# A streaming layer step on one core: state update and difference of two maps at full width, memory products in one stretch

## The chip, the core and the metric

The kernel runs on one core of a Trainium2 chip. The core has a tensor engine (PE in the profile) that multiplies, three engines for elementwise work (VectorE, DVE; ScalarE, ACT; GpSimd, POOL), a sync engine (SP) that here only issues transfers, and 16 transfer engines (DMA). PE multiplies a stationary operand with a moving one: `mm(out, lhsT, rhs)` gives `lhsT`'s columns as the rows of `out`, in a bank of the accumulator memory (PSUM). A product is called full-width here where its result has 128 rows, and narrow where it has 64 or 32; in the profile that is `128*64` or `128*32` ahead of the moving shape. A float32 product is two passes of PE, and `x4` in a row of PE counts passes.

The metric is the device time of one execution in microseconds, the median of the runs.

## The reference

One step of a layer with three groups of heads for 1024 prompt tokens and for 8 batches of 16 decode tokens: differential attention (two softmax maps, the second subtracted with a factor lambda), a matrix memory with gates (mLSTM), and attention into 256 memory tokens. Cut to what the change touches:

```
# differential attention: 4 heads, two maps of 64, values of 128
p = softmax(s)                         # [b, h, map, q, k]
w = p[:, :, 0] - lam * p[:, :, 1]
o = einsum('bhqk,bkhd->bhqd', w, v)
# mLSTM state of a head: 64 x 64 matrix C, vector n; for each chunk
C = decay * C0 + einsum('s,sd,se->de', wS, k, v)
n = decay * n0 + einsum('s,sd->d', wS, k)
# memory attention: 4 heads of 64, 256 memory tokens
om = softmax(qm @ mem_k.T / 8) @ mem_v * silu(gm)
y = x + concat([oa, hb, om]) @ w_out
```

## The kernel before

Tokens lie in 9 tiles of 128: eight of the prompt and one that holds the 8 x 16 decode tokens (`DEC`). The projections run in phases: the four heads of the differential attention, the gates, the memory attention (M), the two head pairs of the mLSTM (B0, B1) and the output projection (O0, O1). A phase loads its weights in k-tiles, splits them in a high and a low part, and `feed` computes a token tile's projection (into banks named z or y) as 24 products of 128x512: `wh` with the high part of the inputs (`hth`), `wh` with their low part (`htl`), `wl` with `hth`. These are most of PE's instructions.

Behind each projection the later stages of the tiles before it are written. `mem_unit` (from L608) is the M stage: queries transposed, scores (`mpm`, L630 to L640), then the part that the change touches, L644 to L666: gates transposed, and for each of two head pairs four transposes of `mpm`, a copy of them to `mpt` by ScalarE (L656), and four products with the memory values `mv` of 64x128. `b_stages` (from L1085) is the mLSTM of a head pair: `mlstm_in`, `mlstm_scores`, the read-out, and the state update (L1105 to L1115): `kw` are the weighted keys of two heads, `vx` their values with a column of ones, `up` the sum that DVE adds to the decayed state `cs`.

The decode attention (`dec_attention`, from L814) runs beside B0 and B1, two steps for each of 8 batches. `scores` loads four key tiles `kc` (512 KB each) and multiplies them with the block-diagonal queries `qz`, 32 rows a head. `values` transposes the exponentials `se` to `ewt`, loads four value tiles `vc` and multiplies, 32 rows a head (head, map, query), copies the sum to `ems`, and a last product with the signed reciprocal sums `sr` subtracts the two maps: 64 rows of `oa` for one batch. `kc` and `vc` share a ring of seven buffers. `mem_decode` (from L912) does the decode tokens' attention into their memories in the phase O0, with key tiles `mkc`.

Nothing of the order is written by hand. Each engine executes its instructions in one order that a scheduler fixes when the program is built, from the code's order, from priorities (`ahead(n)`) and from its own estimates. SP issues transfers in that order, and a transfer that waits for its data holds those behind it. The transfers beside the change are: `mixd`, a tile's finished branch outputs, written to memory by the stages; `bgt`, the gates of a tile, read back; `mb`, a tile of mask rows; the stores of the decode state (`out_11`, `out_12`: L1078, L1079, the second one is the single column `n`) and of the prompt state (L1118, L1119, likewise); and `wraw`, weights as they come from memory.

Of the kernel before, what the change touches and what calls it, by code (L numbers as in the profile page):

```python
# [11 lines left out]
F32 = mybir.dt.float32  # L12
# [20 lines left out]
# columns of the relaid w_in: a head of A: q k v ga; ib fb gb; qm gm; a head pair of B: q k v ob  # L33
W_A, W_G, W_M, W_B = 0, 2048, 2312, 2824

# the phases of the projections: priority of the stages before a tile, of its weights and of its
# products; order of the passes for the first tile and the others; banks; engines of the weights' hi
# parts (even k, odd k); k whose lo part is made by Pool; engine that evacuates transposes
# [15 lines left out]
# steps of the decode attention after each tile of the head pairs of B  # L54
# [4 lines left out]
def hymba_step(ctx: ExitStack, tc: tile.TileContext, a: dict, o: dict):  # L59
# [47 lines left out]
    def bc(ap, n):  # L107
        """[p, ...] -> [p, ..., n], repeated along a new last axis"""
        return ap.unsqueeze(len(ap.shape)).broadcast_to(list(ap.shape) + [n])

    def rep(ap, n):
        """[p, ...] -> [p, n, ...], repeated along a new first free axis"""
        return ap.unsqueeze(1).broadcast_to([ap.shape[0], n] + list(ap.shape[1:]))
# [4 lines left out]
    def flat(ap):  # L118
        return ap.rearrange("p a b -> p (a b)")

    # ------------------------------------------------------------------ constants
# [13 lines left out]
    def rsqrt(dst, ss, n):  # L135
        """dst = (ss + n eps) ** -0.5, the reciprocal rms over sqrt(n); the gains carry sqrt(n)"""
        V.tensor_scalar(ss, ss, n * EPS, None, ALU.add)  # L137
        root(dst, ss)
# [15 lines left out]
    # mixed branch outputs and gates of a token tile, stabilisers, values of the new decode tokens  # L154
# [6 lines left out]
    def small_loads():  # L161
# [3 lines left out]
        # carried here: the roots of n, the halves of silu and sigmoid (written with tanh), and, in  # L165
        # the gain of q, 8 * 0.125 / slope of the next head
# [12 lines left out]
    def selectors():  # L179
        # e16[r, q] = (r % 16 == q); bm[r, b] = (r // 16 == b); par[r, i] = ((r // 16) % 2 == i)  # L180
        # h32[r, h] = (r // 32 == h); selc[r, (h, q)] = h32[r, h] * e16[r, q]
# [5 lines left out]
        # sgn[r] = 1 on the rows of map 0, -lam on those of map 1, rows (h, m, q)  # L187
# [6 lines left out]
    def split_T(src, hi, lo, n):  # L194
        """transpose n [128,128] column blocks of src, split into hi and lo [128, n, 128]"""
# [7 lines left out]
    # the tensor engine's clock rises while the first loads run  # L203
# [9 lines left out]
    def weights(w, c0, n, gain=None, spare=()):  # L213
        """columns c0 to c0 + n of a [1024, .] weight, as hi and lo k-tiles; gain scales its rows.
        spare: (pool, tag, bufs) for raw tiles, where there is room"""
# [67 lines left out]
    def norm_T(xt, xp, hi, lo, xT=None):  # L283
        """rms-normed rows (gain not yet applied), transposed and split"""
# [16 lines left out]
    # a token tile's projection is traced ahead of the later stages of the tiles before it  # L301
# [20 lines left out]
    # -------------------------------------------- memory keys and values  # L322
# [9 lines left out]
    # -------------------------------------------- differential attention, prompt  # L332
# [4 lines left out]
    def a_norm(z):  # L337
        """q and k of a head, both maps, over their rms (gains not yet applied)"""
# [16 lines left out]
    def a_post_dec(h, z):  # L355
        """decode tile: q into block-diagonal (m, d) x (b, m, q) stationaries, k transposed"""
# [22 lines left out]
    def a_post(h, t, z, grp):  # L379
        # dist is scaled by the slope, so the scores carry scale / slope  # L380
# [24 lines left out]
        # contraction over (hi, lo) of q in the first map, (lo, hi) in the second  # L405
# [11 lines left out]
    def a_unit(h, t, grp):  # L417
        """attention of one query tile, in two stages"""
# [29 lines left out]
        # the norm takes out the sum of the first map, but for its eps  # L448
# [23 lines left out]
    # -------------------------------------------- mLSTM gate rows: (tile, head) x token in tile  # L472
    R = 36

    def gate_rows():
        # in buffers of the next phase
# [16 lines left out]
        # decode rows restart at every batch  # L493
# [12 lines left out]
        # log_sigmoid(f) = min(f, 0) - log1p(exp(-|f|)), log1p(u) = 2 atanh(u / (2 + u))  # L506
# [27 lines left out]
        # running stabiliser over the prompt chunks, per head  # L534
# [48 lines left out]
    # -------------------------------------------- cross-attention into the memory  # L583
    def mem_q(z, gt):
        """reciprocal rms of the queries, gate"""
# [10 lines left out]
    def mem_dec_q(z):  # L596
        """decode tile: queries, transposed"""
# [10 lines left out]
    def mem_unit(t, z):  # L608
        # the scores are scaled by the reciprocal rms of q in the softmax; the keys carry q's gain
# [8 lines left out]
        # (hi, lo) of the even heads, (lo, hi) of the odd ones  # L618
# [24 lines left out]
        yield  # L643
        tg = bank("tp").rearrange("p (a k) -> p a k", a=4)  # L644
# [4 lines left out]
        av = bank("av")[:, 0:256].rearrange("p (c k) -> p c k", c=2)  # L649
        for pr in range(2):  # L650
            tp = bank("tp").rearrange("p (a k) -> p a k", a=4)
            for h2 in range(2):
                for kt in range(2):
                    PE.transpose(tp[:, h2 * 2 + kt], pm[:, 2 * pr + h2, kt * P:(kt + 1) * P], ident)
            pt = shp.tile([P, 4, P], F32, tag="wth", name="mpt", bufs=3)
            S.copy(pt, tp)  # L656
            for kt in range(2):
                for h2 in range(2):
                    mm(
                        av[h2 * 64:h2 * 64 + 64, pr], mv[:, kt, pr * 2 + h2], pt[:, h2 * 2 + kt],  # L660
                        kt == 0, kt == 1,
                    )
        # this part of the mixed tile stays transposed
# [43 lines left out]
    # memory keys and values, in buffers that the attention uses later  # L707
    def mem_stages(t):
        def run(z):
# [9 lines left out]
            # 8 of gqm for the 8 that the reciprocal rms of q lacks, times 0.125 of the softmax: none left  # L719
# [63 lines left out]
    # the input and forget gates and gb, behind the last head  # L783
# [27 lines left out]
    # -------------------------------------------- attention over the caches, decode  # L811
    NKD = 1040

    def dec_attention():  # L814
# [16 lines left out]
        oa = ep.tile([P, 4, P], F32, name="oa")  # L831

        def scores(b):
            """rows (h, m, q): exp of the scores over the 1040 keys, signed reciprocal sums"""
# [24 lines left out]
        def values(b, se, sm):  # L859
            sr = ep.tile([P, 64], F32, tag="sr", name="sr", bufs=4)  # L860
            V.tensor_scalar(sr, flat(selc), sm[:, 5:6], None, ALU.mult)
# [27 lines left out]
            # the two maps, weighted and subtracted: rows (h, q)  # L889
            rs = slice((b % 2) * 64, (b % 2) * 64 + 64)  # L890
            mm(avb[rs, P:2 * P], sr, ms)
            S.copy(oa[rs, b // 2, :], avb[rs, P:2 * P])  # L892
# [18 lines left out]
    # -------------------------------------------- attention over the memories, decode  # L911
    def mem_decode(md):  # L912
        """two batches at a time, rows (head, batch of the pair, query)"""
        # contraction over (batch of the pair, head dimension): block-diagonal stationaries
# [48 lines left out]
    # -------------------------------------------- mLSTM  # L963
    # masks over (s, t): prompt causal; decode causal within a batch
# [342 lines left out]
```

## Time and profile before

| | us |
|---|---|
| runs | 783.5, 783.51, 788.57 (median 783.51) |
| profiled execution, span | 774.3 |
| PE busy | 738.2 (95%) |
| DVE, ACT, POOL busy | 473.7, 333.4, 237.4 |
| bytes moved by transfers | 106.19 MB, mean 137 GB/s |

The span is what the profiler sees between the first and the last instruction. The run's time has 9.2 us more around it. A row of the timeline tells the start, the duration (that of a pipelined PE row reaches into the next), the engine, the line, the operation with its result and operands, and how many were joined in the row; in brackets stands the idle time before it and what ended it. For PE the distance from start to start is the better measure of what an instruction costs.

### The profile page before, as it was taken

Reading aid. Unit: us, or ns where it says so; the run is one execution under the profiler, and the core shown is the slowest. Engines: PE = TensorE matmul, PEld = TensorE weight load, DVE = VectorE, ACT = ScalarE, POOL = GpSimd, SP = SyncE. Lnnn points to the kernel's source line nnn. Section 1 sums busy time; section 2 is a strip of 40 time slices with the busy share of each in tenths; the row PEclk is TensorE's granted clock in tenths of the full one; section 3 lists DMA queues with packets and bytes.
Section 4 is the critical chain, followed back from the end, with each engine's and each line's share of the span. In section 5 each row is a group of like instructions: output and inputs, shape, how many; then the busy total and the mean of one; then the engine's idle time right before and its main releaser. Section 6 shows DMA issues by size and latency. Waiting matters only on the chain.

```text
span 774.3 us, 14523 instructions
## 1 busy us (share of the span) xinstructions
PE 738.2 (95%) x4976; PEld 599.9 (77%) x4976; DVE 473.7 (61%) x1466; ACT 333.4 (43%) x976; POOL 237.4 (31%) x332
## 2 busy tenths in 40 slices
PE   7998999999999999999999999899979997799998
PEld 6776788878888888998878776577747775578887
DVE  6788886677787778677575835347335347644111
ACT  6566634564664466555356532234223334200200
POOL 6653441323223223336313502111012036221500
PEclk9999999999999999999999999999989999999999
DMA  8733430151014112324002407979994728874422
GB/s 310 287 107 109 149 89 22 41 157 45 25 49 124 46 35 70 106 76 124 25 15 46 123 14 251 200 276 327 348 207 157 286 42 299 194 260 124 142 83 95
DMA packets 84387, 106.19 MB, mean 137 GB/s; under 512 B 16054, under 2 KB 52698, under 8 KB 84314
## 3 DMA queue, kind: packets, MB, share of 16 engines
q1 hardware_dynamic: 84314, 105.28, 44.2%
q8 instruction: 39, 0.64, 0.3%
q14 instruction: 34, 0.28, 0.1%
HBM read 86.01 MB, written 19.23 MB: 136 GB/s over the span
## 4 chain that ended last, share of the span: by engine, by line
PE 75%; DMA 9%; DVE 9%; issue 2%; ACT 2%; POOL 2%; SPq 0%; POOLq 0%; DVEq 0%; ACTq 0%
PE ps_z L95 39%; PE ps_y L95 15%; PE ps_s L95 9%; PE ps_av L95 5%; DMA kc<-in_kT_dram 4%; PE ps_tp L459 2%; DVE wl L238 2%; DMA mkc<-in_mkT_dram 1%; DMA wraw<-in_w_in_dram 1%; DMA bgt<-gated 1%; PE ps_tp L200 1%; PE ps_tp L867 1%; PE ps_tp L404 1%; DVE xT L294 1%; POOL asm L133 1%
## 5 line engine op out<-in xcount | busy, mean ns | idle before, releaser
L95 PE MATMUL ps_z<-wh,htl 128*128 128x512 f32 (+2 forms) x552 | 214.8, 391 | 0.1
L95 PE MATMUL ps_z<-wh,hth 128*128 128x512 f32 (+2 forms) x552 | 200.2, 394 | 4.4 <-ACT hth L280 2.1
L95 PE MATMUL ps_z<-wl,hth 128*128 128x512 f32 (+2 forms) x552 | 192.1, 387 | 0.0
L95 PEld LDWEIGHTS ps_z<-wh,hth 128*128 128x128 f32 x552 | 103.6, 190 | 25.5 <-ACT hth L280 2.4
L95 PEld LDWEIGHTS ps_z<-wh,htl 128*128 128x128 f32 x552 | 104.7, 190 | 18.9 <-DVE htl L281 0.8
L95 PEld LDWEIGHTS ps_z<-wl,hth 128*128 128x128 f32 x552 | 103.1, 189 | 18.6 <-issue 1.2
L95 PE MATMUL ps_y<-wh,htl 128*128 128x512 f32 (+2 forms) x176 | 65.6, 374 | 0.0
L95 PE MATMUL ps_y<-wh,hth 128*128 128x512 f32 (+2 forms) x176 | 62.9, 378 | 0.3 <-ACT oa L892 0.3
L133 POOL TENSOR_TENSOR asm<-asm,nhalf 128x4 f32<-128x4 f32 x36 | 39.6, 1100 | 74.4 <-DVE asm L137 58.8
L443 ACT ACTIVATE usx<-usx,usm 128x1024 f32<-128x1024 f32 (+7 forms) x64 | 49.7, 778 | 29.0 <-DVE usm L437 26.5
L95 PE MATMUL ps_y<-wl,hth 128*128 128x512 f32 (+2 forms) x176 | 61.3, 378 | 0.0
L238 DVE SCALAR_TENSOR_TENSOR wl<-wraw,gnm,wh 128x512 fp32r<-128x512 f32 (+1 forms) x62 | 47.0, 783 | 4.6 <-ACT wh L231 3.2
L231 ACT ACTIVATE wh<-wraw,gnm 128x512 fp32r<-128x512 f32 (+1 forms) x56 | 38.0, 706 | 18.2 <-DMA wraw<-in_w_in_dram 15.7
L95 PE MATMUL ps_s<-aqk 128*128 128x256 f32 (+1 forms) x160 | 42.0, 288 | 0.9 <-ACT aqk L412 0.9
L437 DVE CUSTOM_DVE_ANT_0 usx<-ps_s,tab 128x512 f32<-128x512 f32 (+3 forms) x64 | 37.0, 587 | 8.9 <-PE ps_s L95 7.5
L133 POOL TENSOR_TENSOR usm<-usm,nhalf 128x1 f32<-128x1 f32 x32 | 19.6, 612 | 72.3 <-DVE usm L467 67.9
L95 PE MATMUL ps_s<-akl,aqk 128*128 128x256 f32 (+1 forms) x160 | 41.0, 283 | 0.0
L95 PE MATMUL ps_av<-avg,wth 128*128 128x128 f32 x288 | 38.7, 276 | 0.2 <-DVE uot L469 0.2
L95 PEld LDWEIGHTS ps_av<-avg,wth 128*128 128x128 f32 x288 | 36.9, 191 | 2.5 <-ACT wth L460 0.6
L95 PEld LDWEIGHTS ps_y<-wh,hth 128*128 128x128 f32 x176 | 32.8, 188 | 5.8 <-ACT oa L892 0.6
L95 PEld LDWEIGHTS ps_y<-wl,hth 128*128 128x128 f32 x176 | 32.9, 188 | 5.5 <-DVE wl L238 0.3
L95 PEld LDWEIGHTS ps_y<-wh,htl 128*128 128x128 f32 x176 | 33.1, 188 | 5.0
(443 smaller groups left out, 1376.7 us busy)
## 6 DMA issues: line engine op xcount, KB each, us to landing
kc<-in_kT_dram SPq DMA_DIRECT2D x32, 512.0 KB, 8.9
vc<-in_cache_attn_v_dram SPq DMA_DIRECT2D x32, 512.0 KB, 6.8
wraw<-in_w_in_dram SPq DMA_DIRECT2D x56, 256.0 KB, 3.0
omx<-mixd SPq DMA_DIRECT2D x9, 512.0 KB, 4.1
out_dram<-oxt SPq DMA_DIRECT2D x17, 256.0 KB, 4.3
xt<-in_x_prompt_dram SPq DMA_DIRECT2D x8, 512.0 KB, 7.7
wraw<-in_w_out_dram SPq DMA_DIRECT2D x16, 256.0 KB, 4.2
oxt<-in_x_prompt_dram SPq DMA_DIRECT2D x16, 256.0 KB, 3.4
```

The source lines that it names most:

```text
L95: PE.matmul(out, lhsT, rhs, start=start, stop=stop)
L133: G.tensor_tensor(dst, ss, nhalf[:, 0:ss.shape[1]], ALU.pow)
L200: PE.transpose(tv[:, i, :], src[:, (c + i) * P:(c + i + 1) * P], ident)
L231: S.activation(wh[:, 0:n], raw[:, 0:n], AF.Copy, scale=g_)
L238: V.scalar_tensor_tensor(wl[:, 0:n], raw[:, 0:n], g_, f(wh[:, 0:n]), ALU.mult, ALU.subtract)
L294: V.scalar_tensor_tensor(xT[:, cs], xT[:, cs], math.sqrt(D), rep(rb, 4), ALU.mult, ALU.mult)
L404: PE.transpose(tp[:, i], flat(nd[:, 2 * i:2 * i + 2]), ident)
L437: V.tensor_tensor_reduce(s_[:, c * 512:c * 512 + w], sp[:, 0:w], tab[:, tx:tx + w], -slope, BIG if c == 0 else sm[:, m:m + 1], ALU.add, AL ...
L443: S.activation(s_[:, 0:nk], s_[:, 0:nk], AF.Exp, bias=last, scale=-1.0, accum_out=sm[:, 4 + m:5 + m])
L459: PE.transpose(tp[:, i], sx[0][:, (c + i) * P:(c + i + 1) * P], ident)
L867: PE.transpose(tp[0:pn, c - c0, :], se[:, c * P:c * P + pn], ident)
```

## The change

Comments are left out of the code, which moves the line numbers, and three things are changed.

In `mem_unit`, the eight transposes of the softmax rows come first, into two tiles `mpt`, copied by ScalarE and by VectorE; then the gates are transposed; then all eight products stand in one stretch.

In `dec_attention`, `sr` becomes two static tiles with 128 columns, one for batches with an even number and one for the odd ones; the other half of each is zero. The products of two batches are made together at the odd one, two full-width products that accumulate, and one copy moves 128 rows to `oa`.

In `b_stages`, the state update of both heads is one product `kw` (128 columns) with `vx` (130 columns). Its result has the two heads' updates on the diagonal and two blocks off it that nobody reads.

```diff
@@ mem_unit
+        av = bank("av")[:, 0:256].rearrange("p (c k) -> p c k", c=2)
+        pts = []
+        for pr in range(2):
+            tp = bank("tp").rearrange("p (a k) -> p a k", a=4)
+            for h2 in range(2):
+                for kt in range(2):
+                    PE.transpose(tp[:, h2 * 2 + kt], pm[:, 2 * pr + h2, kt * P:(kt + 1) * P], ident)
+            pts.append(shp.tile([P, 4, P], F32, tag="wth", name="mpt", bufs=3))
+            copy("SV"[pr], pts[pr], tp)
         tg = bank("tp").rearrange("p (a k) -> p a k", a=4)
...
-        av = bank("av")[:, 0:256].rearrange("p (c k) -> p c k", c=2)
         for pr in range(2):
-            tp = bank("tp").rearrange("p (a k) -> p a k", a=4)
-            for h2 in range(2):
-                for kt in range(2):
-                    PE.transpose(tp[:, h2 * 2 + kt], pm[:, 2 * pr + h2, kt * P:(kt + 1) * P], ident)
-            pt = shp.tile([P, 4, P], F32, tag="wth", name="mpt", bufs=3)
-            S.copy(pt, tp)
             for kt in range(2):
                 for h2 in range(2):
                     mm(
-                        av[h2 * 64:h2 * 64 + 64, pr], mv[:, kt, pr * 2 + h2], pt[:, h2 * 2 + kt],
+                        av[h2 * 64:h2 * 64 + 64, pr], mv[:, kt, pr * 2 + h2], pts[pr][:, h2 * 2 + kt],
                         kt == 0, kt == 1,
                     )
@@ dec_attention
+        srs = []
+        for i in range(2):
+            srs.append(ep.tile([P, 2, 64], F32, name=f"sr{i}"))
+            G.memset(srs[i][:, 1 - i], 0.0)
+        held = []
...
         def values(b, se, sm):
-            sr = ep.tile([P, 64], F32, tag="sr", name="sr", bufs=4)
-            V.tensor_scalar(sr, flat(selc), sm[:, 5:6], None, ALU.mult)
+            sr = srs[b % 2]
+            V.tensor_scalar(sr[:, b % 2], flat(selc), sm[:, 5:6], None, ALU.mult)
...
             S.copy(ms, avb[:, 0:P])
-            rs = slice((b % 2) * 64, (b % 2) * 64 + 64)
-            mm(avb[rs, P:2 * P], sr, ms)
-            S.copy(oa[rs, b // 2, :], avb[rs, P:2 * P])
+            held.append(ms)
+            if b % 2:
+                for i in range(2):
+                    mm(avb[:, P:2 * P], flat(srs[i]), held[i], i == 0, i == 1)
+                held.clear()
+                S.copy(oa[:, b // 2, :], avb[:, P:2 * P])
@@ b_stages
-            up = bank("av")[:, 0:65]
-            for h2 in range(2):
-                mm(up[h2 * 64:h2 * 64 + 64], kw[:, h2], vx[:, h2])
+            up = bank("av")[:, 0:130]
+            mm(up, flat(kw), flat(vx))
...
-                    V.tensor_copy(csn[sl, cc], up[sl])
+                    V.tensor_copy(csn[sl, cc], up[sl, cc])
...
-                        csn[sl, cc], cs[sl, cc], dec[sl, t, pr, 0:1], up[sl], ALU.mult, ALU.add
+                        csn[sl, cc], cs[sl, cc], dec[sl, t, pr, 0:1], up[sl, cc], ALU.mult, ALU.add
```

The scheduler's order changes from the first M stage to the end. Three places follow. The first is PE's queue at a token tile of the memory attention (the first one in the order). Rows with `-` stand there before, with `+` now; `mkh`, `mkl` and `mqs` belong to the scores of the next tile.

```order
 L95 MATMUL ps_z<-wl,hth_122 128x512 x8
+L650 MATMUL ps_tp<-ident,mpm 128x128 x4
 L95 MATMUL ps_s<-mkh,mqs 128x256
 L95 MATMUL ps_s<-mkl,mqs 128x256
 L95 MATMUL ps_s<-mkh,mqs 128x256
+L650 MATMUL ps_tp<-ident,mpm 128x128 x4
```

```order
-L646 MATMUL ps_tp<-ident,mgt 128x128 x2
-L654 MATMUL ps_tp<-ident,mpm 128x128 x8
-L95 MATMUL ps_av<-mpt,mv 64x128 x4
+L655 MATMUL ps_tp<-ident,mgt 128x128 x2
+L95 MATMUL ps_av<-mpt,mv 64x128 x8
 L616 MATMUL ps_tp<-ident,mqn 128x128 x2
-L95 MATMUL ps_av<-mpt,mv 64x128 x4
```

The transposes moved in between the scores, and the two groups of four products became one of eight.

The second place is SP's queue around the store of the decode state in B0 (`out_11`, `out_12`), from the store of the decode tile's mixed rows (`mixd8`) on. This is before:

```order
L843 DMA kc_5914<-in_kT_dram 128x1024
L1042 DMA mixd8_87<-hb_5742 128x128
L991 DMA bgt_5868<-gated2_90 128x128
L843 DMA kc_5920<-in_kT_dram 128x1024
...
L1079 DMA out_12_dram<-C0_5586 128x8x1
L843 DMA kc_6085<-in_kT_dram 128x1024
L1042 DMA mixd0_79<-hb_5843 128x128
L991 DMA bgt_6070<-gated3_91 128x128
L843 DMA kc_6091<-in_kT_dram 128x1024
L843 DMA kc_6099<-in_kT_dram 128x1024
```

And this is the change:

```order
L850 DMA kc_5923<-in_kT_dram 128x1024
...
L1053 DMA mixd8_87<-hb_5742 128x128
...
L1090 DMA out_12_dram<-C0_5586 128x8x1
L1053 DMA mixd0_79<-hb_5842 128x128
L1002 DMA bgt_6069<-gated3_91 128x128
L883 DMA vc_5989<-in_cache_attn_v_dram 128x2x512
L850 DMA kc_6084<-in_kT_dram 128x1024
L850 DMA kc_6090<-in_kT_dram 128x1024
L850 DMA kc_6098<-in_kT_dram 128x1024
```

The fourth key tile moved ahead of the `mixd8` store, and the fifth moved behind the `mixd0` store, `bgt` and a value tile.

The third place is PE's queue at the first value products of the decode attention (`vc,ewt`). This is before:

```order
L95 MATMUL ps_s<-kc,qz 32x256 x4
L95 MATMUL ps_z<-wh,htl_133 128x512
L95 MATMUL ps_z<-wh,hth_124 128x512
L95 MATMUL ps_z<-wh,htl_133 128x512
L867 MATMUL ps_tp<-ident,se 16x128
L996 MATMUL ps_tp<-ident,kg 128x128
L997 MATMUL ps_tp<-ident,bqn 128x128
L95 MATMUL ps_y<-vc,ewt 32x128 x20
```

And this is the change:

```order
L875 MATMUL ps_tp<-ident,se 128x128 x8
L95 MATMUL ps_s<-kc,qz 32x256 x12
L95 MATMUL ps_z<-wh,hth_125 128x512
L95 MATMUL ps_z<-wh,htl_134 128x512
L95 MATMUL ps_av<-vx_5352,kw 128x130
L95 MATMUL ps_z<-wh,hth_125 128x512
L95 MATMUL ps_z<-wh,htl_134 128x512
L95 MATMUL ps_z<-wh,hth_125 128x512
L875 MATMUL ps_tp<-ident,se 16x128
L95 MATMUL ps_y<-vc,ewt 32x128
```

The scores of three key tiles (12 products) now stand ahead of the first value products, where those of one (4 products) stood; a state update is one row of 128x130.

## Rows read from the trace of the kernel before

**Rows 1.** The page's first part: busy us, share of the span, instructions

```profile
PE 738.2 (95%) x4976; PEld 599.9 (77%) x4976; DVE 473.7 (61%) x1466; ACT 333.4 (43%) x976; POOL 237.4 (31%) x332
```

**Rows 2.** Windows: length, busy us (count) by engine, clock, DMA share, GB/s

```profile
470.00:500.00 30.00, 26.24 (x228) 18.71 (x230) 14.56 (x52) 7.44 (x27) 6.45 (x12) 0.94 0.95 247
500.00:560.00 60.00, 60.00 (x620) 43.52 (x613) 30.45 (x104) 19.18 (x56) 6.64 (x9) 1.00 0.89 314
660.00:690.00 30.00, 25.26 (x190) 18.45 (x189) 16.61 (x58) 4.50 (x17) 8.33 (x14) 0.94 0.89 236
```

**Rows 3.** Waits of PE from 470 to 692 us: total us, times, longest us

```profile
PE ps_s L95 <- DMA kc<-in_kT_dram: 7.0, 3, 3.2
PE ps_s L95 <- DMA mkc<-in_mkT_dram: 3.9, 1, 3.9
PE ps_s L95 <- DVE mb L1015: 2.2, 1, 2.2
```

**Rows 4.** Timeline of SP's queue: start us, us to issue, what is issued

```profile
479.59 2.06 SPq L1079 DMA_DIRECT2D out_dram<-C  x1
...
481.75 3.28 SPq L843 DMA_DIRECT2D kc<-in_kT_dram  x1
485.13 0.37 SPq L1042 DMA_DIRECT2D mixd<-hb  x1
```

**Rows 5.** The chain that ended last: start us, us, what

```profile
481.75 13.02 DMA kc<-in_kT_dram
```

**Rows 6.** Timeline of PE: start us, us, instruction, count [idle before, releaser]

```profile
479.13 0.64 PE L95 MATMUL ps_s<-kc,qz 128*32 128x256 f32 x8 [1.07 <-DMA kc<-in_kT_dram]
...
494.90 0.64 PE L95 MATMUL ps_s<-kc,qz 128*32 128x256 f32 x8 [2.70 <-DMA kc<-in_kT_dram]
...
497.69 0.65 PE L95 MATMUL ps_y<-vc,ewt 128*32 128x128 f32 x8
...
574.26 1.06 PE L95 MATMUL ps_s<-kc,qz 128*32 128x256 f32 x2 [3.19 <-DMA kc<-in_kT_dram]
```

**Rows 7.** Windows of two stretches behind the store of 479.59

```profile
486.00:488.00 2.00, 2.00 (x14) 1.63 (x14) 1.36 (x5) 0.49 (x3) 0.00 (x0) 1.00 0.69 41
488.00:490.00 2.00, 2.00 (x15) 1.74 (x14) 1.62 (x6) 1.37 (x6) 1.10 (x2) 1.00 1.54 111
```

**Rows 8.** Timeline of PE: sixteen narrow passes, and one state update among z products

```profile
475.95 0.69 PE L95 MATMUL ps_av<-vx,km 128*64 128x65 f32 x16
476.56 0.64 PE L95 MATMUL ps_s<-kc,qz 128*32 128x256 f32 x8
...
480.74 0.39 PE L95 MATMUL ps_z<-wh,hth 128*128 128x512 f32 x1
481.06 0.34 PE L95 MATMUL ps_av<-vx,kw 128*64 128x65 f32 x4
...
481.66 0.39 PE L95 MATMUL ps_z<-wh,hth 128*128 128x512 f32 x1
481.89 0.40 PE L95 MATMUL ps_z<-wh,htl 128*128 128x512 f32 x1
```

**Rows 9.** Timeline of PE: a 128x130 product of the read-out and its follower

```profile
561.30 0.39 PE L95 MATMUL ps_s<-cs,qk 128*128 128x130 f32 x2
561.53 0.45 PE L95 MATMUL ps_s<-vx,mb 128*128 128x65 f32 x3
```

**Rows 10.** Timeline of PE: two groups of memory products, with and without a wait

```profile
390.21 0.66 PE L654 MATMUL ps_tp<-ident,mpm 128*128 128x128 f32 x4
390.97 0.66 PE L95 MATMUL ps_av<-mpt,mv 128*64 128x128 f32 x8
...
425.94 0.84 PE L95 MATMUL ps_z<-wl,hth 128*128 128x512 f32 x3
426.71 0.66 PE L95 MATMUL ps_av<-mpt,mv 128*64 128x128 f32 x8
427.30 0.50 PE L95 MATMUL ps_z<-wl,hth 128*128 128x512 f32 x1
```

## The prediction

> **What bounds the kernel now.** First the page's busy times: the tensor engine (PE) is busy for 738.2 us, 95% of a span of 774.3 us, so nearly every microsecond of work taken from it could be a microsecond of time [rows 1]. Next, where the missing 36 us lie. The stage table shows that from 500 to 560 us, in the middle of the decode attention, PE has no idle time at all, while 470 to 500 us has 3.8 us of it and 660 to 690 us 4.7 us [rows 2]. In those stretches the transfers keep 0.89 to 0.95 of their engines busy. The list of waits names what PE waited for: three cache key tiles (kc), 7.0 us, one tile of memory keys (mkc), 3.9 us, and one mask tile (mb), 2.2 us [rows 3]. So the changed part (memory attention, state update, decode attention) is bound by PE's own work, broken by a few waits that end with a transfer. The prediction needs both: what PE's work loses, and whether those waits give it back.
>
> The waits have a common cause. On the sync engine's (SP's) queue the store of the decode state's last column (4-byte pieces, line 1079) is issued at 479.59 us and alone takes 2.06 us to issue; the next kc is issued at 481.75, and PE gets it only at 494.90 [rows 4, 6]. The chain of waits has that transfer as 13.02 us [rows 5]. Meanwhile the transfers move 41 to 111 GB/s, against 247 over the whole stretch [rows 2, 7]. Later PE is idle again for 3.19 us, until a kc at 574.26 [rows 6], whose issue stands behind the store of the prompt state's last column.
>
> **State update.** Two half-width products (64x65) become one full-width product (128x130), 16 times (8 prompt tiles, 2 pairs). Each half product is two passes, and one update now stands as four passes. From the z product at 480.74 to the one at 481.66 are 0.92 us; two z products take 0.23 each (481.66 to 481.89), so the update costs 0.92 - 0.46 = 0.46 us [rows 8]. Sixteen such passes in a row, with leaving them, last 0.61 us (475.95 to 476.56), so four are at most 0.15 us of work, and at least 0.31 us of the 0.46 is what PE pays to leave the full width and come back [rows 8]. The new product has two full-width passes; the 128x130 product of the read-out takes 0.23 (561.30 to 561.53) [rows 9]. In a stretch of its own an update thus falls from 0.46 to 0.23.
>
> **Memory attention.** Eight half-width products of a token tile stood in two groups of four, and now stand in one. The work is the same; one departure from full width is saved where the groups stood apart. A group costs 1.36 - 0.69 = 0.67 us (425.94 to 427.30, less three z products) [rows 10]. The first group also waited for ScalarE's copy of the transposes where nothing stood between: 390.97 - 390.21 = 0.76 us for four transposes of 0.109, so some 0.2 to 0.3 us of waiting beside the switch [rows 10]. Five groups of before show it, and all the transposes now stand ahead: 5 x 0.24 = -1.2 us. The second copy moves to VectorE, which is 61% busy and has room [rows 1].
>
> **Difference of the maps.** Eight half-width products of 128x128 become four pairs of full-width ones, four copies fewer go to ScalarE, and ems of an even batch is held for one batch more. One half product is two passes of 128 columns, a pair of full products four; two half products never stood together, so a pair replaces four passes by four, and only departures are saved. The zeroing is two writes on POOL at the start of the decode attention, hidden under PE's full stretch.
>
> **Departures, counted over the whole order.** Single prices would count too much: many updates stood next to other narrow products, and the moved products now cut some 32-wide runs in two. From the memory attention to the end the old order leaves full width 89 times (45 for 32-wide, 44 for 64-wide products), the new one 67 times (51 and 16). So 22 x 0.31 = -6.8 us. Against this stand the longer passes of the update, 16 x (0.23 - 0.12) = +1.7 us. With the waits for ScalarE, PE's work changes by -6.8 + 1.7 - 1.2 = **-6.3 us**.
>
> There is a rule that speaks against this. The passes of two half products start together: four passes of 65 columns come at the price of two. The Trainium skill, "TensorE: Matmul & The Clock Gate", Part 3 (packing small matmuls), says that products on different strips of the array run concurrently and that this is the remedy for small ones; by it alone the update would only lose. A sum by that rule has +1.7 us where mine has -5.1; the row of the single update, 0.46 us against two passes of 0.23 in all, is against it.
>
> **What the waits do.** The scheduler also moves transfers.
> (a) Four kc in place of three now stand ahead of the store of the decode tile's mixed rows (mixd8). PE's first kc wait (1.07 us [rows 6]) loses its cause: -1.1.
> (b) kc5 to kc7 now stand behind the state's store, behind the mixd0 store, which was issued at 485.13, and behind one more value tile; and PE takes all three in one row (12 products) ahead of the first value products, where before it needed one kc. Before, value products began at 497.69 [rows 4, 6]. One more 512 KB tile ahead of them is 0.524 MB / 247 GB/s = 2.1 us [rows 2]; and PE comes 1.1 us earlier by (a), which it waits here. +3.2; bounds 0 (everything, the stores too, comes earlier with PE) and +14.6 (rival C).
> (c) The last mkc stands behind one more weight tile: 0.262 MB / 236 GB/s = 1.1 us [rows 2]. PE already waits for it: +1.0, bounds 0 and 1.1.
> (d) At the end of the second pair bgt4 moves ahead of the stores and bgt5 behind them: the mb wait of 2.2 us [rows 3] may go, or come one tile later: 0, bounds -2.2 and +2.2.
> Sum: -6.3 - 1.1 + 3.2 + 1.0 = **-3.2 us**, so a profiled span of about 771. The runs' median of before is 783.51, 9.2 above its profiled span, so the time is about **780 us**.
>
> **Rivals.**
> A: the waits move with PE, since the stores that cause them hang on PE's products, and nothing is given back; (d) may bring up to 2.2 more. -6.3 - 1.1 = -7.4 to -9.6: 774 to 776 us. For it: from 500 to 560 PE does not wait although the transfers are at 0.89. Against: kc5 really stands behind more than it did.
> N: the change does not do what it says for PE: the cost beside a narrow product is not one of leaving full width, or is merely moved to the 32-wide runs that are cut (45 to 51). Then +1.7 remains, and (b) adds up to 2.1: 785 to 787 us. For it: the concurrent passes. Against: the 0.46 us of a single update.
> C, slower: kc5 to kc7 in the shadow of the state's store. If the slow stretch lasts beyond kc5, which lands 13.0 us after about 485.5, and kc6 and kc7 come at the mean of 41 and 111 GB/s, 6.9 us each [rows 7], the first values begin at 485.5 + 13.0 + 13.8 = 512.3, 14.6 after 497.7. Sum: -6.3 - 1.1 + 1.1 + 14.6 + 1.0 = +9.3: 793 us. It decides when kc7 lands more than about 12 us later against PE's work than it did. Against: before, kc6 and kc7 came soon after kc5, PE's value products beginning 2.8 us after it.
>
> **How the numbers follow.** The forecast (partly given back, 776 to 783) has 0.47, A 0.27, N 0.14, C 0.12. The median of before is read to some 1% (7.8 us), about what a measurement of this kernel can tell from no change: faster is below 775.7, slower above 791.3. Faster is A, 0.27; slower is C, 0.12; the rest, 0.61, is the same. The range 771 to 788 takes in N and most of A, with the bounds of (c) and (d); it leaves out C (0.12), the far end of A (0.06) and little of N (0.02).
>
> **What would show it.** In the new profile: (1) state updates as one product of two passes, about 0.23 us between z products without a slow neighbour; (2) the memory groups as 16 passes in a row, and no wait for ScalarE ahead of them; (3) PE busy time some 5 to 6 us less than 738.2; (4) no kc wait at the fourth kc, a longer one, 4 to 6 us, ahead of the first value products; (5) the later kc wait of 3.2 us still there, behind the prompt state's store; (6) the mkc wait at 4 to 6 us. The prediction is wrong if PE's work falls by clearly more or less than 5 to 6 us, or if the sum of the kc waits stays at 7 us (then A) or passes 15 us (then C).

## The result: 0.7% slower

The changed kernel takes 790.76 us in the median of ten runs (787.73 to 793.95), the kernel before 783.5 us (781.59 to 788.57). The ratio, taken over all runs, is 1.0074, with a 95% interval of 1.0049 to 1.0099; the two medians alone would give 1.0093. Forecast were 780 us and a range of 771 to 788; the sign was wrong too, though 1.0074 is still "within 1%".

The page of the changed kernel, its waits of PE, and two windows where the clock fell (columns as in [rows 1], [rows 3] and [rows 2]):

```profile
PE 743.0 (94%) x4944; PEld 606.3 (77%) x4944; DVE 478.9 (61%) x1474; ACT 328.6 (42%) x964; POOL 236.7 (30%) x334
```

```profile
PE ps_s L95 <- DMA kc<-in_kT_dram: 8.7, 4, 6.6
PE ps_z L95 <- DVE mgt L593: 3.6, 4, 2.3
PE ps_s L95 <- DVE esm L857: 2.8, 2, 2.3
PE ps_s L95 <- DVE mb L1026: 2.0, 1, 2.0
PE ps_s L95 <- DMA mkc<-in_mkT_dram: 0.7, 1, 0.7
```

```profile
582.00:590.00 8.00, 8.00 (x36) 5.54 (x37) 2.97 (x12) 1.78 (x4) 0.00 (x0) 0.64 1.01 391
655.00:660.00 5.00, 2.69 (x11) 2.08 (x10) 3.18 (x9) 1.94 (x10) 4.69 (x6) 0.50 1.04 399
```

PE executes 32 passes fewer and is nevertheless 4.8 us longer busy: the mean granted clock fell from 0.989 to 0.976. After its long waits PE runs at a mean clock of 0.50 to 0.64 for some microseconds, and at half the clock (1.2 GHz) z products start 0.43 us apart (664.22 to 664.65) in place of 0.23. Each of its five stretches at that clock behind 400 us begins in a wait of PE or right behind one. Beside the waits that answer to [rows 3] there are new ones: for the evacuation of a gate in the memory attention (L593) and for VectorE in the decode attention (esm).

The growth of the profiled span, 12.7 us, can be split: 7.9 us are PE's longer idle time (44.0 against 36.1). If each busy microsecond of PE is weighted with the clock granted in it, PE's work is 723.2 us at full clock, against 725.1 before; what the lower clock adds to it rose from 13.1 to 19.8 us. So 7.9 + 6.7 - 1.9 = 12.7. Against a second trace of the kernel before (the first experiment below) the same split is 9.7 + 4.1 - 1.6 = 12.2. These are estimates from single executions; in the stretch up to 380 us, where nothing was changed, the weighted work scatters over 4 us (356.8 to 361.2) in all the traces.

The span is 787.0 us in an execution that took 788.78. So only 1.8 us lie around a span. The 9.2 us that the prediction put there were then mostly the difference between a quick execution of some 776 us, which had been profiled, and the median of the runs.

### The profile page after: what moved, and what is told of

It is laid out like the page before. It is cut to its first block, busy times and chain, and to the rows that moved or that the text cites. A ratio compares the mean times of both kernels' runs of the same rounds, so it can differ in the third digit from the quotient of the medians.

```text
span 787.0 us, 14462 instructions
## 1 busy us (share of the span) xinstructions
PE 743.0 (94%) x4944; PEld 606.3 (77%) x4944; DVE 478.9 (61%) x1474; ACT 328.6 (42%) x964; POOL 236.7 (30%) x334
## 4 chain that ended last, share of the span: by engine, by line
PE 70%; DMA 13%; DVE 9%; issue 2%; ACT 2%; POOL 2%; SPq 1%; DVEq 0%; POOLq 0%; ACTq 0%
PE ps_z L95 36%; PE ps_y L95 14%; PE ps_s L95 9%; PE ps_av L95 4%; DMA kc<-in_kT_dram 3%; DMA bgt<-gated 3%; DMA wraw<-in_w_in_dram 2%; PE ps_tp L459 2%; DMA vc<-in_cache_attn_v_dram 1%; DMA mvc<-in_cache_mem_v_dram 1%; DVE wl L238 1%; PE ps_tp L875 1%; PE ps_tp L404 1%; PE ps_tp L200 1%; DVE xT L294 1%
## 5 line engine op out<-in xcount | busy, mean ns | idle before, releaser
L95 PE MATMUL ps_z<-wl,hth 128*128 128x512 f32 (+2 forms) x552 | 195.8, 393 | 0.0
L95 PE MATMUL ps_y<-wh,htl 128*128 128x512 f32 (+2 forms) x176 | 67.5, 385 | 0.0
L95 PE MATMUL ps_y<-wh,hth 128*128 128x512 f32 (+2 forms) x176 | 65.5, 393 | 0.0
```

Source lines behind the costliest of these rows:

```text
L95: PE.matmul(out, lhsT, rhs, start=start, stop=stop)
```

## What the prices did

The prices of the single edits came out as worked out, where they stand between full-width products. A state update between z products (as in [rows 8]), and a memory stretch (as in [rows 10]), timeline of PE of the changed kernel:

```profile
391.95 0.38 PE L655 MATMUL ps_tp<-ident,mgt 128*128 128x128 f32 x2
392.26 1.09 PE L95 MATMUL ps_av<-mpt,mv 128*64 128x128 f32 x16
393.29 0.44 PE L616 MATMUL ps_tp<-ident,mqn 128*128 128x128 f32 x2
...
484.43 0.39 PE L95 MATMUL ps_z<-wh,hth 128*128 128x512 f32 x1
484.66 0.38 PE L95 MATMUL ps_av<-vx,kw 128*128 128x130 f32 x2
484.80 0.48 PE L95 MATMUL ps_z<-wh,htl 128*128 128x512 f32 x1
485.11 0.39 PE L95 MATMUL ps_z<-wh,hth 128*128 128x512 f32 x1
```

From 484.43 to 485.11 are 0.68 us; less two z products of 0.23, the update costs 0.22 us where it cost 0.46. Sixteen memory passes take 1.03 us, where two groups of eight took 0.59 each ([rows 10], 426.71 to 427.30) and one departure more. Five of the eight token tiles have their sixteen passes in one row; in the other three the scheduler still put two groups of eight. The rest is around them: three stalls of PE, and what they wait for.

Two of them in the timeline of PE: the first is in the memory attention and answers to nothing of before, where the same place waited 0.4 us; the second answers to [rows 6], 574.26:

```profile
436.11 1.20 PE L95 MATMUL ps_z<-wh,hth 128*128 128x512 f32 x4 [2.28 <-DVE mgt L593]
...
581.92 1.08 PE L95 MATMUL ps_s<-kc,qz 128*32 128x256 f32 x8 [6.65 <-DMA kc<-in_kT_dram]
```

The wait for the key tile behind the prompt state's store doubled, from 3.19 to 6.65 us. Not all of that is lost, for the kernel before has a pause shortly ahead of its wait that the changed kernel has not:

```profile
569.15 0.62 PE L95 MATMUL ps_s<-kc,qz 128*32 128x256 f32 x3 [1.25 <-issue]
```

The third is at the end of the second pair. On SP's queue (columns as in [rows 4]) bgt now stands behind the store of 4-byte pieces (L1090), and in the chain (as in [rows 5]) it takes 13.19 us, in which VectorE waits 6.91 us:

```profile
635.76 0.58 SPq L1090 DMA_DIRECT2D out_dram<-C  x1
636.45 0.69 SPq L1053 DMA_DIRECT2D mixd<-hb  x1
637.19 0.44 SPq L1002 DMA_DIRECT2D bgt<-gated  x1
```

```profile
637.19 13.19 DMA bgt<-gated
```

```profile
650.47 0.29 DVE L1005 SCALAR_TENSOR_TENSOR bgt<-bth,bgt 128x128 f32<-128x128 f32 x1 [6.91 <-DMA bgt<-gated]
```

Compared with a second trace of the kernel before (the first experiment below), by the start of the first product of every projection tile, the changed kernel falls 4 us behind in the memory attention, has made that good at 470 us, falls 7 us behind between 505 and 549 us and 7 more between 620 and 661 us. The order around these tiles differs, so part of this is work that moved. PE's idle time and the time that the clock added, taken together and against the first trace, grew by 4.5 us from 380 to 470 us, 2.4 from 505 to 549, 1.9 from 549 to 592 (0.9 against the second trace) and 5.4 from 620 to 661.

## Experiments

Theory 1: the memory edit costs the time, by VectorE's second copy. Theory 2: the new order of transfers costs it. Theory 3, formed on the way: the stores of the states' n columns in 4-byte pieces hold up whatever transfer stands behind them, and take back what PE saves. Each kernel was timed in turn with the kernel before on the same chip; the ratios are to that. The runs come from several sessions on different chips, in which the kernel before took 779.2 to 786.3 us, so ratios of different sessions are compared only roughly.

### The same code once more

No edit.

> The kernel before with the changed one's line numbers and no other edit, to have a second trace of it beside the runs it is timed against. Theory 1 (VectorE's second copy holds the projection's bank in the memory attention) and theory 2 (the new order of transfers costs the time at the end of the second head pair) both expect a ratio of 1.00 within 0.4%. If the profile of before was an ordinary execution, its span is again 773 to 776 us; if that execution was a quick one, the span is 779 to 785 us, and the transfer waits (kc, mb, mkc: 13.1 us there) are the part that differs.

Measured: 1.0019 (0.9992 to 1.0047), span 774.8 us in the profiled execution, against a median of 780 us: this execution too is a quick one, the shortest of its ten. The waits are those of [rows 3]:

```profile
PE ps_s L95 <- DMA kc<-in_kT_dram: 6.5, 3, 3.4
PE ps_s L95 <- DMA mkc<-in_mkT_dram: 3.6, 1, 3.6
PE ps_s L95 <- DVE mb L1015: 2.0, 1, 2.0
```

So they stand in both executions.

### One edit at a time

Each of the three parts of the diff alone, the rest as before.

> Only the memory attention is changed (products in one stretch, second copy on VectorE). Theory 1: PE waits for the gate's evacuation (L593) and for the second copy in this phase, 4 to 5 us as in the changed kernel, against some 3.5 us less PE work: ratio 1.000 to 1.008, and the phase's end no earlier than before. Theory 2: the phase gains its 3 to 4 us, ratio 0.995.

Measured: 1.0096 (1.0058 to 1.0135).

> Only the state update is changed. PE's price of an update falls from 0.46 to 0.22 us, 16 times: -3.8 us of PE work. Theory 1: nothing in this edit loads VectorE, so the time falls by 2 to 4 us, ratio 0.995 to 0.998. Theory 2: the scheduler's new order of transfers takes it back or more at the end of the second pair: ratio 1.000 to 1.008, with a longer wait for mb or bgt near 635 to 660 us.

Measured: 1.0030 (1.0004 to 1.0057).

> Only the difference of the maps is changed (four pairs of full-width products). Theory 1: departures saved, some 1 us, ratio 0.997 to 1.001. Theory 2: a loss of some us by the reordered transfers, ratio 1.002 to 1.008, seen as longer kc or bgt waits.

Measured: 1.0000 (0.9977 to 1.0022).

The memory edit alone loses as much as the whole change. The state update is not faster. Sixteen times the price of a single one would be 3.8 us less work, but four of the sixteen stood beside narrow products, and PE's weighted work did not fall in this trace (724.9 us, 724.8 in the second trace of before). Its kc waits are 10.2 us in all, 3.7 more than in the second trace. The maps do nothing that can be measured.

```diff
-            copy("SV"[pr], pts[pr], tp)
+            copy("SS"[pr], pts[pr], tp)
```

> Only the memory attention is changed, and both copies of the transposes are ScalarE's. Theory 1a (VectorE's second copy of 0.69 us stands in its queue ahead of the gate's evacuation that frees the projection's bank): the waits for L593 and for mpt fall from 3.8 us to under 1 us, the phase ends 3 us earlier than in the kernel before, ratio 0.994 to 0.999. Theory 1b (the order of transposes and gates, not the engine of the copy): the waits stay at 3 to 4 us and the ratio at 1.005 to 1.011.

Measured: 1.0081 (1.0050 to 1.0113). Theory 1a falls: without VectorE's copies the edit loses as much. The waits of PE up to 480 us:

```profile
PE ps_z L95 <- DVE mgt L593: 2.7, 2, 2.2
```

The long wait for L593 is still there. The gate's evacuation stands in VectorE's queue behind weight work (L233, which waits for a weight to land) and behind the previous tile's result (L667), and both engines' variants have it so. Why the new order costs it there, no run separates. With either copy there is a second stall, later, in the decode attention; the timeline of PE, first with VectorE's copy:

```profile
494.47 0.49 PE L95 MATMUL ps_av<-vx,kw 128*64 128x65 f32 x4 [3.85 <-DVE cs L1116]
```

and with ScalarE's:

```profile
494.99 0.34 PE L95 MATMUL ps_av<-vx,kw 128*64 128x65 f32 x4 [3.41 <-DVE cs L1116]
```

VectorE is late there since it waits 8.06 us (4.89 with ScalarE's copy) for bgt, which stands behind the decode state's store. That led to theory 3.

> Difference of the maps and state update changed, memory attention as before. If the edits add up, the ratio is 1.003 (update alone 1.003, maps alone 1.000). Theory 2 (the order of transfers at the end of the second pair takes the time): 1.003 to 1.010, with bgt and mb waits of 3 us or more between 635 and 665 us. If PE's saved work came through, 0.994 to 0.997.

Measured: 0.9966 (0.9937 to 0.9995). Two edits of 1.000 and 1.003 make a gain of 0.3% together: the edits don't add up. Each one moves the order of transfers, and that is the likely reason, though no run holds the order fixed. Theory 2 is too simple as well: the same kind of reordering goes with a loss here and a gain there, and what it changes is who stands behind a store.

### The n columns as rows

The decode state's column (128 partitions, 8 batches) is transposed on PE and stored as 8 rows of 512 bytes, the prompt state's as one row of 512 bytes.

```diff
-        SY.dma_start(
-            out=o["s_n"][0, :, hs].rearrange("b h (d o) -> (h d) b o", o=1), in_=C0[:, :, 64:65]
-        )
+        nt = bank("tp")
+        PE.transpose(nt[0:8, 0:P], C0[:, :, 64], ident)
+        nrow = flat(bw.tile([P, 2, 64], F32, tag="bqn", name="nrow", bufs=nb))[0:8]
+        S.copy(nrow, nt[0:8, 0:P])
+        SY.dma_start(out=o["s_n"][0, :, hs].rearrange("b h d -> b (h d)"), in_=nrow)
```

> The kernel before, with the n columns of both states transposed on PE and stored as rows (8 pieces of 512 bytes, one of 512 bytes, in place of 1024 and 128 pieces of 4 bytes); 4 transposes more. Theory 3 (the stores of 4-byte pieces hold up the key tiles behind them): the kc waits fall from 6.5 to 7 us to under 3, the mb wait of 2.0 us too, ratio 0.990 to 0.996. Rival (key tiles are late because they are issued late or because buffers come free late): the waits stay, ratio 0.998 to 1.004.

Measured: 0.9919 (0.9892 to 0.9946), 773.51 us. The kc waits are gone from the list of waits from 470 to 692 us, and so is mkc. At its head now stands:

```profile
PE ps_av L95 <- DVE C L1076: 3.2, 2, 2.2
PE ps_tp L996 <- ACT kg L986: 2.8, 2, 2.0
PE ps_tp L200 <- DMA omx<-mixd: 2.0, 1, 2.0
PE ps_s L95 <- DVE mb L1015: 1.1, 2, 0.7
```

The transfers show why. This is the transfers' view of the kernel before from 478 to 500 us, in 40 slices of 0.55 us: the engines' busy share in tenths, and the rate.

```profile
DMA  9999999999986999567999935415999999989986
GB/s 272 294 358 350 384 406 358 363 327 344 259 170 104 42 23 52 30 52 82 119 156 60 37 22 22 34 54 179 314 347 369 439 406 418 357 317 278 256 367 235
```

For some 9 us (sixteen slices) the engines are at 0.1 to 0.9 and more but move 22 to 170 GB/s. With the columns as rows the store is issued earlier, at 474.06 us, so the stretch that answers to it is 472 to 494 us:

```profile
DMA  9637899799989989999999969799989899992000
GB/s 410 238 89 180 212 177 288 268 394 326 368 337 296 136 177 264 324 376 398 410 417 403 371 223 161 156 365 402 451 335 223 186 320 372 425 410 82 0 0 0
```

Behind the store it moves 136 GB/s and more until the tiles have landed, and then has nothing to do.

The three parts of the change on top of this, one, two or all of them:

> Maps and update changed, n columns stored as rows. Theory 3: PE's saved work (4 us) is then no longer taken back by the key tiles, so the time falls below that of the rows alone by 2 to 4 us: ratio 0.985 to 0.993. Rival: as maps and update without the rows, 1.000 to 1.005.

Measured: 0.9787 (0.9747 to 0.9827), 764.38 us, more of a gain than expected.

> The kernel before with the n columns stored as rows and only the memory attention changed (second copy on VectorE). Of the edit's loss of 7 us alone, two parts are seen: 4 to 5 us of waiting for L593 in the memory attention itself, and 4 us where PE waits for VectorE at 490 to 494 us because VectorE waits for bgt behind the 4-byte stores. Theory 3: the second part goes, the first stays, so beside the rows alone (0.992) the edit is worth between -1 and +3 us: ratio 0.990 to 0.996. Rival (the loss lies in the memory attention and in the schedule it leads to, whatever the stores are): 0.998 to 1.003.

Measured: 0.9898 (0.9862 to 0.9935), 771.3 us.

> The whole change with the n columns stored as rows. Theory 3: without the 4-byte stores the whole change is a gain of 8 to 14 us against the kernel before: ratio 0.980 to 0.990, PE busy under 738 us, kc waits under 2 us; but behind the version without the memory edit (0.979), since the waits for L593 remain. Rival: 0.995 to 1.002.

Measured: 0.9810 (0.9770 to 0.9850), 763.32 us. The whole change, a loss of 0.7% with the 4-byte stores, is a gain of 1.1% without them (0.981 against 0.9919, 763.3 against 773.5 us). PE is busy for 730.9 us, where the rows alone had 741.7 (x4982, clock 0.987; here 0.993). By the weighting above, 5.5 us of this is less work (726.4 to 720.9) and 5.3 us a higher clock, so about half of the gain is the clock's:

```profile
PE 730.9 (96%) x4950; PEld 601.0 (79%) x4950; DVE 479.3 (63%) x1474; ACT 329.2 (43%) x970; POOL 236.3 (31%) x334
```

> The whole change with the n columns stored as rows and both copies of the transposes by ScalarE. If VectorE's copy is a part of the wait for L593, this is 1 to 3 us faster than the same with VectorE's copy: ratio 0.975 to 0.985. If it is not (the memory edit alone measured 1.008 with either engine), the two agree within 1 us.

Measured: 0.9876 (0.9829 to 0.9922), 768.63 us: not better with ScalarE's copies, rather worse; this expectation was wrong. The part of theory 1 that names VectorE's copy has no run left for it; that the memory edit costs time beside the 4-byte stores (1.0096) stands.

> The kernel before with the n columns stored as rows and only the state update changed. The price of an update in the trace says -3.8 us of PE work; without the 4-byte stores nothing takes it back: ratio 0.984 to 0.989, against 0.992 of the rows alone. Rival (the update's gain is lost to the schedule anyway, as it was alone with 1.003): 0.991 to 0.996.

Measured: 0.9771 (0.9749 to 0.9793), 768.63 us, on a chip on which the kernel before had 786.31. The update that gained nothing alone gains beyond the rows' 0.9919. The size is rough, as the two are of different sessions: 1.5% by the ratios, 0.6% by the times (768.63 against 773.51 us). By the times that is about the price of sixteen updates; by the ratios, which lie below what was expected (0.984 to 0.989), it is more than their work, and the rest would have to come from the waits or the clock.

The memory edit is worth little in this company: 0.9898 against 0.9919 of the rows alone, 0.9810 against 0.9787 beside the other two edits. The intervals overlap. In every trace with this edit PE waits for L593 (2.6 to 3.9 us), about what the edit was to save.

That a changed order is a matter of luck remains a rival to theory 3. Against it stands how the kernels part: the six with both columns as rows lie at 0.9771 to 0.9919, the eight with both in pieces at 0.9960 to 1.0096, and the two below with one column of each kind in between.

### Which store, and by what

```diff
-        SY.dma_start(
+        G.dma_start(
             out=o["s_n"][0, :, hs].rearrange("b h (d o) -> (h d) b o", o=1), in_=C0[:, :, 64:65]
         )
```

The prompt state's column likewise.

> The kernel before, with the 4-byte stores of the n columns issued by POOL's queue in place of SP's; the pieces are the same. Theory 3a (the pieces hold the transfer engines, which all queues share): kc, mb and bgt come as late as before, ratio 0.997 to 1.004, and the rate falls under 60 GB/s for some 8 us behind the store again. Theory 3b (the store holds up SP's queue, in which it stands ahead of the key tiles): the kc waits fall under 3 us, ratio 0.988 to 0.996.

Measured: 0.9960 (0.9929 to 0.9992), with the pieces on POOL's queue. The transfers' view of 478 to 500 us:

```profile
DMA  9999999999999999989799996689999999989861
GB/s 369 331 309 387 372 384 356 298 343 372 297 247 98 68 40 72 52 30 66 83 122 70 108 76 63 115 194 273 410 423 383 387 350 375 339 211 267 336 246 45
```

The rate falls to 30 to 122 GB/s for as long as before. So the transfers themselves are held up, whichever queue issued the pieces (3a). The kc waits are shorter all the same, 3.4 us, near what 3b expected, and the time has half of the rows' gain (0.4 of 0.8%). 3b's range ends at the measured ratio, 3a's begins inside its interval. Whether this half comes from a freer SP queue or from the order that changed with it stays open.

> The whole change with only the decode state's n column stored as rows (1024 pieces of 4 bytes less for each pair); the prompt state's 128 pieces stay. Theory 3 by count of pieces: most of the loss hangs on the decode state's column, so the ratio is 0.981 to 0.990, near the 0.981 of both stored as rows. Theory 3c (each store costs the same 8 us, however few its pieces): half of the gain, 0.992 to 1.000.

Measured: 0.9931 (0.9907 to 0.9955).

> The whole change with only the prompt state's n column stored as rows (128 pieces of 4 bytes less for each pair). Theory 3 by count of pieces: little changes, ratio 1.002 to 1.008, and the kc wait of 6 to 7 us near 575 to 582 us stays. Theory 3c (each store costs the same): 0.990 to 0.999, and that wait goes.

Measured: 0.9922 (0.9893 to 0.9951).

Against the whole change's 1.0074 the one store is worth 1.4%, the other 1.5%, both together (0.981) 2.6%. So the prompt state's 128 pieces cost this kernel as much as the decode state's 1024: theory 3c, by the time of the kernel. The waits show which is whose. With only the decode state's column as rows, the timeline of PE still has

```profile
576.82 1.08 PE L95 MATMUL ps_s<-kc,qz 128*32 128x256 f32 x8 [6.46 <-DMA kc<-in_kT_dram]
```

and with only the prompt state's, the kc waits of the whole stretch from 470 to 692 us are

```profile
PE ps_s L95 <- DMA kc<-in_kT_dram: 2.2, 3, 1.4
```

## Why the prediction was wrong

Two steps failed: the count of departures in PE's work, and "What the waits do".

**PE's work** (-6.3 us) is not what the changed kernel shows. The sum takes 89 and 67 departures from full width. These are the narrow stretches counted by width: where 32-row products follow 64-row ones, full width is left once and counted twice. In the traces, from 380 us on, PE comes back to full width 76 times before and 65 times in the changed kernel. At the prediction's 0.31 us that is -3.4 us in place of -6.8; if a change between two narrow widths costs half a departure, the 32 changes of width fewer (175 to 143) make it -5.0. Measured by the weighted work are -1.9 us (-1.6 against the second trace), where the prediction without its waits for ScalarE has -5.1. Between the rows alone and the rows with the whole change the work does fall by 5.5 us, but there PE comes back to full width 82 and 60 times. Given the scatter of some 4 us, neither number is sharp. The rule of packing (rival N) has the row of the single update against it, 0.22 us in place of 0.46. N's weaker form, that the cost is merely moved to the 32-wide runs (45 to 51), is in part borne out. As to the sum by that rule, +1.7 us, no run shows it alone.

**The step that failed most is "What the waits do".** Its sum gave back +3.2 + 1.0 us after a gain of 1.1. Measured in the profiled executions are 7.9 us more of idle PE (9.7 against the second trace) and 6.7 us (4.1) for a lower granted clock, a term that the prediction does not have. By the medians of the runs the loss is 7.3 us. The prediction saw a cause: it named the stores, their 4-byte pieces, the fall of the rate and the 13.02 us. It then costed the change by asking which transfers stand behind the first store, and took the other stores as they were.
(a) was right: no kc wait at the fourth tile.
(b) mis-sized and misplaced. The wait at the first values is not for kc but for VectorE (esm, 2.3 us), which waits for bgt behind the same store:

```profile
498.76 0.29 DVE L1005 SCALAR_TENSOR_TENSOR bgt<-bth,bgt 128x128 f32<-128x128 f32 x1 [4.61 <-DMA bgt<-gated]
```

A transfer of 64 KB held PE up where three of 512 KB were feared to.
(c) was wrong: the mkc wait fell to 0.7 us; PE came to that tile late, at 687.3 us, where it had come at 672.8.
(d) was set to 0 with bounds of 2.2 us to both sides. bgt5 behind the store cost PE 2.0 us for mb at once and, with the waits through VectorE and the inputs of the output projection and a clock of 0.50 behind them, some 5 us until 661 us (7 by the starts of the tiles). I took the next tile's slack for cover, though nothing in the rows showed any. This alone is larger than the forecast gain.
The p_n store was named only as standing where it did ("the later kc wait of 3.2 us still there"); it became 6.65, a net loss of 1 to 2 us.

**The memory attention.** "VectorE is 61% busy and has room" was the wrong question. A share of the span says nothing of an in-order queue at one place: PE needs the bank that L593 frees, and L593 stood behind work that waits for a weight. Some 3.7 us saved (the waits of 1.2 and up to eight departures of 0.31) became waits of 3.6 us in the changed kernel, and 1.7 us more by the lower clock behind them (from 437.6 us). The prediction has no wait in this phase, and the stores have no part in it: with the columns as rows 3.2 and 3.3 us of it remain. That the copy's engine is not the cause, as I thought after the result, the run with ScalarE's copies showed.

**The rivals.** C had one right mechanism, the shadow of the store, but the wrong victim: it watched kc5 to kc7. That its time (793 us) lies nearest is luck, as the wait that it adds up did not come and others made up for it. Its chance of 0.12 was small beside a chain that has four transfers of 8.4 to 13.0 us between 480 and 680 us, one of them in [rows 5]. A (everything comes through) is nearest to what happens when the stores are mended: 0.981 in place of 0.992.

**What should have shown it:** (1) showed; (2) in five tiles of eight, with a wait for VectorE's copy (0.7 us) in place of ScalarE's; (3) did not, as the lower clock hid the little that was saved; (4) partly, for esm and bgt; (5) twice as long; (6) no. Of the signs of being wrong, the one on PE's work came, and the one on the kc waits (7 or 15 us) did not: they sum to 8.7 us, since the losses went to other waits.

## What to carry to other kernels

When the chain of waits goes through transfers that land late for one shared cause, saved engine work can be given back there; mend that cause first and see whether the saved work shows (here a gain of 1.1%, about half of it through the clock, in place of a loss of 0.7%). Price a wait of PE with the lower clock that follows it. Where a scheduler orders the queues, each edit can change them all: ask not which transfer stands behind the slow one in the new order, but what every transfer that could stand there would cost. And ask of an engine that takes over work not how busy it is in the mean but what stands ahead in its queue where someone waits for it.

## What the runs showed of the hardware

Transfers that were issued behind a store of single 4-byte elements landed 9.4 to 13.2 us later in the chains of the two kernels (bgt 9.35 and 13.19 us, where its median is 2.9; kc 13.02 and 12.29). In the trace of the kernel before, which has a record of every packet, the pieces themselves take about 9 ns each, but packets of 4096 bytes that start from 486 to 492 us, behind the decode state's pieces, take 0.5 to 1.9 us on average, and single ones 3.2 us, where the median of the execution is 0.16. Behind the prompt state's pieces a packet of 1024 bytes took 5.7 us (median 0.05). The rate falls there too; the transfers' view of the kernel before from 560 to 574 us, in slices of 0.35 us:

```profile
DMA  9996412101899990038086340332499969999999
GB/s 456 398 402 221 118 44 65 15 3 41 102 97 91 88 3 0 0 9 18 3 9 6 3 6 0 6 9 9 26 79 70 105 132 328 342 369 392 388 398 396
```

So 64 elements on each of two stores do about what 1024 do. Issued by another engine's queue the pieces lower the rate just the same. Why a handful of them is enough, no run here settles.

Of PE, the row of the single update agrees with what the Trainium skill, "TensorEngine Tiling (Array Packing)", Key Properties, says of changing the tiling mode (it drains the engine): a narrow stretch among full-width products cost some 0.31 us beside its passes there.

The version with rows and the whole change (763.3 us) and that with rows, maps and update (764.4 us) are both faster than either kernel.
